# A macaron block on one core: operand and weight tiles 32 bytes further along from one tile to the next

## The chip, the cores and the metric

The kernel runs on one core of a Trainium2 chip. TensorE (PE) multiplies, VectorE (DVE) and ScalarE (ACT) do the element-wise work, GpSimd (POOL) does next to nothing here, and SyncE (SP) issues nearly all transfers. Data lies in SBUF, 128 partitions with one row of bytes each; a tile of 1,024 float32 takes 4,096 bytes of every partition's row. Matmul results go to PSUM, in banks of 512 float32 a partition. The metric is the device time in microseconds (us) of one execution; a lower one is better.

## What is computed

One layer of a streaming encoder, for 1,024 tokens of width 1,024, all in float32:

```python
h = x + 0.5 * swiglu_ffn(rmsnorm(x, norm_ffn1), ffn1_w_in, ffn1_w_out)     # D_FF = 2816
proj = rmsnorm(h, norm_mix) @ w_in                                         # q, k, v, g, p, two gates
ret = retention(rotary(q), rotary(k) * 256**-0.5, v)                       # 4 heads of 256, chunks of 64
ret = ret * rsqrt(mean(ret * ret) + eps) * silu(g)
pool_out = multiscale_pool(p, pool_w, pool_scale)                          # windows 2, 4, 8, 16
merged = sigmoid(gate0 + b0) * (ret @ w_ret_up) + sigmoid(gate1 + b1) * (pool_out @ w_pool_up)
h = h + merged @ w_out
h = h + 0.5 * swiglu_ffn(rmsnorm(h, norm_ffn2), ffn2_w_in, ffn2_w_out)
out = rmsnorm(h, norm_final)
```

## The kernel before

**Products in three parts.** [...] `split` writes the high part with ScalarE (L151) and the low part with VectorE (L152). A product of two operands is three matmuls that add up in one bank (`mm3`, L169 to L173): high weights by high data, high weights by low data, low weights by high data. In every one of them TensorE first loads a block of 128 x 128 of the stationary operand (the rows PEld LDWEIGHTS), while the matmul before it runs, and then streams the moving operand, 512 or 256 columns wide, past it. The trace names lines 171, 172 and 173 for the three.

**Where operands lie.** One pool, `sb`, holds everything that rotates; a tag is a row of equal buffers in it, and a new tile takes a buffer of its tag that has come free. The tags lie in SBUF one behind the other in the order in which they are first used. `mv` (L107, 28 buffers) holds moving operands: high part in the first half of the tile, low part in the second. `wt` (L110, 5 buffers) holds stationary ones, again both parts, each of four blocks of 128 columns. `raw` (4) holds weights as loaded, `t4` (9) and `tl` (4) results and spilled data, all of 4,096 bytes; `c2` (8) holds halves of 2,048 bytes. Some operands lie elsewhere: the blocks that `Next.blocks` (L337) makes for the lower level of the product scheme go to `tl` or `t4` as its callers say (L622), and `scores` (L1403) and the state of the retention put theirs into `t4`. In front of `sb` lies the pool `cp` with constants: among others the zeros and `ones_r`, a block of ones for sums over partitions.

**Fewer products.** A 2 x 2 scheme with seven products in place of eight (`strassen`) runs over all large products; pairs of neighbouring groups share a second level (`common`, L521). The groups read operands T and R of the normed input and weights L and S of sums of weight blocks, which VectorE and ScalarE prepare just ahead. In `prod` (L451, L543) the weights' tile stays over four (or two) steps and the moving tile changes with every step of three matmuls. In the second half of an FFN (`ffn_out`, `step`, L863) one weights' tile and one moving tile serve twelve matmuls.

**Order.** `Flow` runs a list of steps: each has a preparation and a body, and preparations run four steps (`LOOK`) ahead. Work that nobody waits for at once (scaling, gates, norms) stands in a second queue, of which one or two pieces are let in after each body. Each engine works through its instructions in the order that comes out of this; semaphores order the engines among each other.

**The zeros.** At the start VectorE fills `zero` (L187), and TensorE runs twelve matmuls on it (L193), which set the two banks that sums use and keep TensorE going while the first loads are on their way.

## Time and profile before

| | us |
|---|---|
| median of 3 runs | 2163.72 |
| lowest and highest | 2162.26, 2164.65 |
| span of the profiled execution (its time from the first to the last instruction) | 2160.9 |
| PE busy in it | 2148.0, 10,668 matmuls |
| DVE busy | 1870.0, 3,300 instructions |
| ACT busy | 1088.9, 2,047 instructions |

The profile is of one execution of its own. Its span leaves out what lies before the first and behind the last instruction, and is 2.8 us below the median. Busy time is the time in which an engine has an instruction; matmuls are pipelined, and each row gives a longer duration (0.39 us for 512 columns) than the distance to the next start. The distance between starts, from the view in order of time, tells how fast TensorE works. The first FFN fills the span to about 640 us, the projections go to about 1170, retention and pooling to about 1370, the branches' last products and the output product to about 1520, and the second FFN fills the rest.

### The profile page before, as it was taken

What the parts mean: (1) busy time and instruction counts of PE and PEld (TensorE: products, weight loads), DVE (VectorE), ACT (ScalarE), POOL (GpSimd) and SP (SyncE); (2) the same over time, 40 slices, a digit from 0 to 9 for tenths busy, and PEclk for the clock granted to TensorE, in tenths of its full rate; (3) what the DMA queues carried; (4) which work ended last, traced back from release to release, by engine and by line L of the source; (5) the groups of instructions that cost most, each with busy time, mean ns of one, the idle gap of its engine ahead of it and who ended that gap; (6) DMA issues with size and microseconds to landing.
All of it is one profiled execution on the core that took longest, in us unless ns stands there. A gap on an engine that the chain in (4) does not pass through costs nothing.

```text
span 2160.9 us, 29697 instructions
## 1 busy us (share of the span) xinstructions
PE 2148.0 (99%) x10668; PEld 1816.9 (84%) x10668; DVE 1870.0 (87%) x3300; ACT 1088.9 (50%) x2047; POOL 0.2 (0%) x4
## 2 busy tenths in 40 slices
PE   9999999999999999999999999999999999999998
PEld 7888888888888888888888898887888888888887
DVE  8799899998788798899767877899999989999784
ACT  8544444545656444444426754446644444455463
POOL 0000000000000000000000000000000000000000
PEclk9999999999999999999999999999999999999999
DMA  7232323596323333333485567624133232359532
GB/s 261 69 129 104 101 93 127 165 339 207 122 93 107 109 127 108 118 107 119 153 268 191 167 224 256 218 97 160 65 117 103 98 107 99 118 185 334 178 122 78
DMA packets 117828, 320.92 MB, mean 149 GB/s; under 512 B 12976, under 2 KB 17200, under 8 KB 117680
## 3 DMA queue, kind: packets, MB, share of 16 engines
q1 hardware_dynamic: 117104, 317.97, 43.4%
q8 instruction: 83, 1.36, 0.3%
q10 hardware_dynamic: 576, 1.05, 0.1%
q14 instruction: 65, 0.53, 0.1%
HBM read 228.27 MB, written 90.70 MB: 148 GB/s over the span
## 4 chain that ended last, share of the span: by engine, by line
PE 90%; DVE 7%; ACT 1%; issue 1%; DMA 1%; SPq 0%; ACTq 0%; DVEq 0%
PE c_b L171 2%; PE c_b L173 2%; PE c_b L172 2%; PE a_b L173 2%; PE a_b L171 2%; PE a_b L172 2%; PE c_e L173 2%; PE c_e L171 2%; PE c_e L172 2%; PE a_e L173 2%; PE a_e L171 1%; PE a_e L172 1%; PE bp6b L172 1%; PE bp6b L173 1%; PE bp6b L171 1%; PE c_a L172 1%
## 5 line engine op out<-in xcount | busy, mean ns | idle before, releaser
L172 PE MATMUL c_b<-n3T,c_wS 128*128 128x512 f32 x176 | 68.5, 389 | 0.0
L173 PE MATMUL c_b<-n3T,c_wS 128*128 128x512 f32 x176 | 68.5, 389 | 0.0
L171 PE MATMUL c_b<-n3T,c_wS 128*128 128x512 f32 x176 | 68.2, 390 | 0.0
L171 PE MATMUL a_b<-n1T,a_wS 128*128 128x512 f32 x168 | 65.5, 390 | 0.0
L172 PE MATMUL a_b<-n1T,a_wS 128*128 128x512 f32 x168 | 65.4, 389 | 0.0
L173 PE MATMUL a_b<-n1T,a_wS 128*128 128x512 f32 x168 | 65.4, 389 | 0.0
L173 PE MATMUL a_a<-n1R,a_wL 128*128 128x512 f32 x120 | 46.7, 390 | 0.8 <-DVE a_wL L152 0.8
L171 PE MATMUL a_a<-n1R,a_wL 128*128 128x512 f32 x120 | 46.8, 390 | 0.0
L172 PE MATMUL a_a<-n1R,a_wL 128*128 128x512 f32 x120 | 46.7, 389 | 0.0
L172 PE MATMUL c_a<-n3R,c_wL 128*128 128x512 f32 x112 | 43.7, 390 | 0.0
L171 PE MATMUL c_a<-n3R,c_wL 128*128 128x512 f32 x112 | 43.6, 389 | 0.0
L173 PE MATMUL c_a<-n3R,c_wL 128*128 128x512 f32 x112 | 43.6, 389 | 0.0
L173 PEld LDWEIGHTS c_b<-n3T,c_wS 128*128 128x128 f32 x176 | 33.0, 188 | 6.9
L171 PEld LDWEIGHTS c_b<-n3T,c_wS 128*128 128x128 f32 x176 | 33.0, 188 | 6.9
L172 PEld LDWEIGHTS c_b<-n3T,c_wS 128*128 128x128 f32 x176 | 33.0, 188 | 6.8
L171 PEld LDWEIGHTS a_b<-n1T,a_wS 128*128 128x128 f32 x168 | 31.5, 188 | 6.8 <-ACT a_v L471 0.3
L173 PEld LDWEIGHTS a_b<-n1T,a_wS 128*128 128x128 f32 x168 | 31.5, 188 | 6.6
L172 PEld LDWEIGHTS a_b<-n1T,a_wS 128*128 128x128 f32 x168 | 31.5, 188 | 6.5
L173 PE MATMUL c_e<-n3T,c_wS 128*128 128x512 f32 x88 | 35.1, 399 | 0.4 <-DVE c_wS L152 0.4
L171 PE MATMUL c_e<-n3T,c_wS 128*128 128x512 f32 x88 | 34.5, 393 | 0.0
L172 PE MATMUL c_e<-n3T,c_wS 128*128 128x512 f32 x88 | 34.4, 391 | 0.0
L173 PE MATMUL a_e<-n1T,a_wS 128*128 128x512 f32 x84 | 33.4, 398 | 0.9 <-DVE a_wS L152 0.9
(3058 smaller groups left out, 8076.2 us busy)
## 6 DMA issues: line engine op xcount, KB each, us to landing
c_ra<-in_f_in SPq DMA_DIRECT2D x22, 512.0 KB, 3.6
c_rb<-in_f_in SPq DMA_DIRECT2D x22, 512.0 KB, 4.1
a_ra<-in_f_in SPq DMA_DIRECT2D x21, 512.0 KB, 3.6
a_rb<-in_f_in SPq DMA_DIRECT2D x21, 512.0 KB, 4.4
t<-au SPq DMA_DIRECT2D x11, 512.0 KB, 2.6
b<-ag SPq DMA_DIRECT2D x11, 512.0 KB, 2.7
r<-au SPq DMA_DIRECT2D x11, 512.0 KB, 3.6
br<-r SPq DMA_DIRECT2D x11, 512.0 KB, 5.4
```

What stands on the lines that cost most here:

```text
L171: mm(dst, w[0], m[0], start=start, stop=False, skip_group_check=True)
L172: mm(dst, w[0], m[1], start=False, stop=False, skip_group_check=True)
L173: mm(dst, w[1], m[0], start=False, stop=stop, skip_group_check=True)
```

## The change

Tiles of `mv` and `wt` are allocated as rows of 1,032 float32 and used without the last eight, so that each buffer starts 4,128 bytes behind the one before it instead of 4,096: 32 bytes further along in a line, if the row of bytes is thought of as cut into lines of a power of two. The five places that take tiles of these tags go through one new function. The zeros move from a tile of their own in `cp` to a buffer of `c2`, which makes room for the extra bytes; as the first tile asked of `sb` they also put `c2` in front of the other tags. A tile of 32 bytes, `line`, is set aside in `cp` and never used. No other instruction is added, removed or moved in the program's text.

```diff
+    def staggered(tag, bufs, dtype, name):
+
+        return sb.tile([P, S + 8], dtype, tag=tag, bufs=bufs, name=name)[:, :S]
+
     def mv(name):
-        return sb.tile([P, 2, H], F32R, tag="mv", bufs=N_MV, name=name)
+        return staggered("mv", N_MV, F32R, name).rearrange("p (z c) -> p z c", z=2)
 
     def wt(name):
-        return sb.tile([P, 2, 4, P], F32R, tag="wt", bufs=N_WT, name=name)
+        return staggered("wt", N_WT, F32R, name).rearrange("p (z i c) -> p z i c", z=2, i=4)
...
-    zero = cp.tile([P, H], BF16, name="zero")
+    zero = sb.tile([P, 2 * H], BF16, tag="c2", bufs=N_C2, name="zero")[:, :H]
     nc.vector.memset(zero, 0.0)
...
     ones_r = cp.tile([P, P], F32R, name="ones_r")
+    cp.tile([P, 8], F32, name="line")
...
-                store[k // 2] = sb.tile([P, S], F32, tag="mv", bufs=N_MV, name=f"{name}{n}{k}")
+                store[k // 2] = staggered("mv", N_MV, F32, f"{name}{n}{k}")
...
-                self.row = sb.tile([P, S], F32, tag="mv", bufs=N_MV, name=f"{self.name}row")
+                self.row = staggered("mv", N_MV, F32, f"{self.name}row")
...
-                o = self.rows[n] = sb.tile([P, S], F32, tag="mv", bufs=N_MV, name=f"{self.name}o{n}")
+                o = self.rows[n] = staggered("mv", N_MV, F32, f"{self.name}o{n}")
```

## The prediction

> **What bounds the kernel now.** I read the page first (busy times, clock, chain), then the waits of TensorE, then the order of time of single matmuls, because the pitch from one matmul's start to the next is what this change can move.

> ```profile
> span 2160.9 us, 29697 instructions
> PE 2148.0 (99%) x10668; PEld 1816.9 (84%) x10668; DVE 1870.0 (87%) x3300; ACT 1088.9 (50%) x2047; POOL 0.2 (0%) x4
> PEclk9999999999999999999999999999999999999999
> PE 90%; DVE 7%; ACT 1%; issue 1%; DMA 1%; SPq 0%; ACTq 0%; DVEq 0%
> ```

> TensorE is busy 99% of the span, its clock is granted in full in all 40 slices, and it makes up 90% of the chain that ended last. The waits of TensorE are small; these are the longest:

> ```profile
> PE set L193 <- DVE zero L188: 1.2, 1, 1.2
> PE a_e L173 <- DVE a_wS L152: 0.9, 2, 0.5
> PE a_a L173 <- DVE a_wL L152: 0.8, 1, 0.8
> ```

> So the time is the number of matmuls times their pitch. A busy PE is not PE at its peak, so the pitch has to be read from starts. First 512 columns wide, in FFN 2 (time from the span's start, duration, instruction):

> ```profile
> 1604.89 0.39 PE L171 MATMUL c_a<-n3R,c_wL 128*128 128x512 f32 x1
> ...
> 1607.16 0.39 PE L172 MATMUL c_a<-n3R,c_wL 128*128 128x512 f32 x1
> ```

> Ten pitches in 2.27 us: 227 ns (226.7 over longer stretches). Now 256 columns wide; a row each at the start of a group and where it ends:

> ```profile
> 1592.50 0.28 PE L171 MATMUL c_b<-n3R,c_wx 128*128 128x256 f32 x1
> ...
> 1593.22 0.28 PE L171 MATMUL c_x<-n3R22y,c_ws 128*128 128x256 f32 x1
> ...
> 1593.94 0.28 PE L171 MATMUL c_b<-n3R,c_ws 128*128 128x256 f32 x1
> ...
> 1594.66 0.29 PE L171 MATMUL c_b<-n3R22y,c_wy 128*128 128x256 f32 x1
> 1594.78 0.28 PE L172 MATMUL c_b<-n3R22y,c_wy 128*128 128x256 f32 x1
> 1594.90 0.28 PE L173 MATMUL c_b<-n3R22y,c_wy 128*128 128x256 f32 x1
> 1595.02 0.28 PE L171 MATMUL c_b<-n3R22y,c_wy 128*128 128x256 f32 x1
> ...
> 1595.36 0.28 PE L171 MATMUL c_x<-n3R22y,c_ws 128*128 128x256 f32 x1
> ...
> 1596.04 0.39 PE L171 MATMUL c_e<-n3T,c_wL 128*128 128x512 f32 x1
> ```

> From 1592.50 to 1594.66 there are 18 pitches in 2.16 us: 120 ns. From 1595.36 to 1596.04 there are six in 0.68 us: 113 ns. The two groups named c_x<-n3R22y have the same line, shapes and engine, and differ in one thing: the moving operand. Line 622 puts the block y2, which the group at 1593.22 reads, into a buffer of the tag tl, and y3 and y4, read from 1594.66 on, into buffers of t4. In the program as built, counting bytes within a line of 128, every buffer of mv, wt, tl and c2 starts at 32, and every one of t4 and raw at 96. So where the moving operand and the weights that are loaded meanwhile lie at the same place of a line, a matmul of 256 columns takes 120 ns, and where they lie 64 bytes apart, 113.

> The difference of 512 and 256 columns at the same place is 226.7 - 120 = 106.7 ns for 256 columns, so both widths hold the same remainder that isn't columns: 120 - 106.7 = 13.3 ns a matmul, and half of it, 6.7, at 64 bytes apart. This remainder is what the change can reach.

> **The change part by part.**

> *The steps of 32 bytes.* Buffers of mv and wt become 4128 bytes instead of 4096. With five buffers of wt and 28 of mv, worked out in the order in which the tags are first used, wt starts at 64, 96, 0, 32, 64 and mv at 96, 0, 32, 64 and round again; t4, raw and c2 start at 0, tl at 96. Offsets inside a tile are multiples of 512 bytes and change nothing. Put on the trace's order of matmuls, buffers as they are now, the moving operand and the next weights are then 0, 32, 64 and 96 bytes apart in about a quarter of the cases each; today 8,041 matmuls of 512 columns are practically all at 0, and of 2,334 of 256 columns four fifths. (The count by width is mine from the trace; it agrees with the page: if all 10,668 were one or the other, 2148.0 us would need 8,136 wide ones.)

> What 32 and 96 bytes cost is not in the trace, nor is a settled 512 at 64. Bounds of the remainder: 0 and 13.3 ns. I take 6.7, the only row that isn't at the same place, for all three. Then the mean remainder is (13.3 + 3 x 6.7) / 4 = 8.3. The wide ones gain 5.0 ns: 8,041 x 5.0 = 40.2 us. The narrow ones go from a mean of 118.6 to 115.0: 8.4 us. Sum: 48.6 us faster if every matmul runs at its settled pitch.

> *Settling.* It won't: the trace shows what a change of place costs. In the rows below two matmuls read ones_r (at 96) between operands at 32.

> ```profile
> 1557.00 0.39 PE L172 MATMUL c_e<-n3T,c_wL 128*128 128x512 f32 x1
> 1557.23 0.39 PE L173 MATMUL c_e<-n3T,c_wL 128*128 128x512 f32 x1
> 1557.45 0.62 PE L238 MATMUL n30b<-n30dg,ones_r 128*128 128x512 f32 x2
> 1557.91 0.40 PE L171 MATMUL c_b<-n3R,c_wS 128*128 128x512 f32 x1
> 1558.15 0.39 PE L172 MATMUL c_b<-n3R,c_wS 128*128 128x512 f32 x1
> 1558.38 0.40 PE L173 MATMUL c_b<-n3R,c_wS 128*128 128x512 f32 x1
> 1558.61 0.39 PE L171 MATMUL c_b<-n3R,c_wS 128*128 128x512 f32 x1
> 1558.84 0.39 PE L172 MATMUL c_b<-n3R,c_wS 128*128 128x512 f32 x1
> ```

> From 1557.23 to 1558.84 seven pitches take 1.61 us, where seven settled ones take 1.587: 23 ns for two changes, 12 each. After the change the distance alters some 3,450 times, about every third matmul (the moving tile changes with i in prod, L451): at most 3,450 x 12 = 41 us. At least nothing: at 1594.66 the move to 64 bytes apart costs no more than 120 ns for three matmuls and gains from the fourth. I take 15 us, a good third: most of the excess lies behind a return to the same place, which is one change in four, and the steps of FFN out, with one pair of tiles for twelve matmuls (step, L863), settle. Left: 33.6 us.

> *VectorE.* When TensorE gets faster, VectorE is late next. It is nearly full in two stretches:

> ```profile
> 1400.00:1650.00 250.00, 248.93 (x1141) 206.27 (x1140) 244.27 (x432) 138.52 (x253) 0.00 (x0) 1.00 0.30 104
> 1900.00:2000.00 100.00, 100.00 (x481) 84.28 (x481) 97.05 (x167) 51.16 (x93) 0.00 (x0) 1.00 0.79 274
> ```

> (Columns: stretch, length, busy PE, PEld, DVE, ACT.) In the first, VectorE has 5.7 us free of 250, and a gain of 1.6% would ask for 3.9 of them; queues rarely use all, so I take off 2 us there and 1 in the second. Nothing is lost if it keeps pace, at most the 6 us that both stretches would gain. VectorE's and ScalarE's own instructions don't get slower by place: the same shape takes

> ```profile
> L152 DVE TENSOR_TENSOR c_wS<-c_S,c_wS 128x512 fp32r<-128x512 f32 x46 | 31.4, 685 | 1.2 <-ACT c_wS L151 1.2
> L716 DVE TENSOR_TENSOR cu<-cu,n3rb 128x512 f32<-128x512 f32 x44 | 30.1, 685 | 0.0
> L151 ACT CAST a_wS<-a_S 128x512 fp32r<-128x512 f32 x45 | 27.1, 620 | 13.3 <-PE a_a L173 5.0 <-DVE a_S L429 3.7 <-PE a_e L173 2.5
> L151 ACT CAST a_wL<-a_ra 128x512 fp32r<-128x512 f32 x30 | 18.4, 621 | 17.6 <-PE a_e L173 5.6 <-DVE ag L710 4.8 <-DMA a_ra<-in_f_in 2.6
> ```

> with all operands at 32, all at 96, or a mix: 685 and 620 ns either way.

> *The zeros and the empty line.* The same memset and twelve warm-up matmuls write and read another address. Cost 0: the twelve end near 6.5 us under the first loads, and c2 is first wanted again later. Without that cover a wait for the buffer would cost at most the 1.2 us of the first wait above. The tile called line takes no instruction. Order and number of all other instructions stay, so queues and transfers move only with TensorE; no transfer is among TensorE's waits.

> Sum, against the span: -48.6 + 15 + 3 = -31 us, to 2130; the median of the runs lies 2.8 us above the span, so 2133.

> [...]

> **The rivals.**

> *The beat is lost (slower).* Today all operands lie alike, and TensorE falls into a steady 226.7 ns. If distances that change every third matmul keep it unsettled, the pitch is that of the rows from 1557.23 on, 1.61 / 7 = 230 ns: 8,041 x 3.3 = 27 us more, the narrow ones staying at 120: 2190. For it: the seven rows; against it: 113 ns once settled. It decides as soon as the mean pitch of the wide ones, unsettled, is above 226.7.

> *Only the narrow ones respond.* No settled 512 at another place is in the trace. Then 8.4 us: 2155.

> *VectorE becomes the bound.* If TensorE gains but waits for weights through FFN 1 and FFN 2, half of 31 us is left: 2148. Against it: three waits of under 1 us with VectorE at 98%.

> *The change does nothing.* The 7 ns come from something else than place, such as the traffic on the tag's buffers: 2163.7. Against it: same line, same shape, 2 us apart.

> **How the numbers follow.** Forecast 0.55, narrow alone 0.14, VectorE 0.06, nothing 0.05, beat lost 0.20. Below and above 0.2% (4.3 us, about what a measurement of this kernel can tell from no change): faster 0.75, same 0.05, slower 0.20. The forecast's own range is 2100 to 2158. With a remainder of 0 at the three other places and no settling cost the time is near 2065 (10 ns on each wide one, 8.6 on each narrow one), with 12 ns for every change and no gain 2205; from 2098 to 2176 about 2 in 10 is left out.

> **What would show it.** In the changed kernel's order of time, 512-wide starts less than 226.7 ns apart, mixed values inside a group of twelve, settled ones in the steps named bp and dp; 256-wide ones near 115; busy VectorE above 98% from 1400 on and TensorE's waits on L152 longer. Wrong: starts 230 ns apart and wandering (beat lost), or 226.7 throughout (place without effect).

## The result and the profile after

The changed kernel takes 2201.4 us (median of 4 runs, 2200.26 to 2201.88) against 2162.99 for the kernel before on the same chip (2161.79 to 2164.65): a ratio of 1.0173, interval 1.0159 to 1.0188. It is 38 us slower; the forecast was 2133, 31 us faster.

From the page of the changed kernel: span, busy times, the granted clock in 40 slices, and the chain's shares by engine.

```profile
span 2199.7 us, 29697 instructions
PE 2186.0 (99%) x10668; PEld 1816.3 (83%) x10668; DVE 1876.4 (85%) x3300; ACT 1089.9 (50%) x2047; POOL 0.2 (0%) x4
PEclk9999999999999999999999999999999999999999
PE 95%; DVE 3%; DMA 1%; ACT 1%; issue 0%; SPq 0%; DVEq 0%; ACTq 0%
```

The counts of instructions are those of before and the granted clock is 0.999, as before; PE's busy time went from 2148.0 to 2186.0 us, nearly as much as the span (2160.9 to 2199.7). The waits of TensorE are as small as they were (engine, tile and line | what it waited for | us in total, times, longest):

```profile
PE set L197 <- DVE zero L192: 1.2, 1, 1.2
PE a L175 <- ACT n1R L159: 0.8, 1, 0.8
PE a_a L177 <- DVE a_wL L156: 0.8, 1, 0.8
```

So the matmuls themselves follow one another more slowly. In the order of time (start, duration, instruction) the group c_a<-n3R,c_wL in the second FFN has 48 matmuls of 512 columns; first the kernel before, its first start and the first start of the group that follows, then the changed kernel:

```profile
1601.49 0.39 PE L171 MATMUL c_a<-n3R,c_wL 128*128 128x512 f32 x1
...
1612.38 0.39 PE L171 MATMUL c_e<-n3T,c_wS 128*128 128x512 f32 x1
```

```profile
1591.88 0.39 PE L175 MATMUL c_a<-n3R,c_wL 128*128 128x512 f32 x1
...
1603.00 0.40 PE L175 MATMUL c_e<-n3T,c_wS 128*128 128x512 f32 x1
```

10.89 us and 11.12 us: 226.9 and 231.7 ns a matmul. The narrow groups that the prediction read, in the changed kernel:

```profile
1621.84 0.28 PE L175 MATMUL c_x<-n3R22y,c_ws 128*128 128x256 f32 x1
...
1622.56 0.28 PE L175 MATMUL c_b<-n3R,c_ws 128*128 128x256 f32 x1
...
1623.95 0.28 PE L175 MATMUL c_x<-n3R22y,c_ws 128*128 128x256 f32 x1
...
1624.65 0.40 PE L175 MATMUL c_e<-n3T,c_wL 128*128 128x512 f32 x1
```

Six of 256 columns take 0.72 and 0.70 us, 120 and 117 ns; before it was 120 and 113.

Over the whole span I took the distance from each matmul's start to the next in the order of time (distances above 260 and 150 ns, which are pauses, left out) and set beside it the addresses of the program as built. "Distance" below is the start of the moving operand less the start of the weights that are loaded meanwhile, those of the next matmul, counted within 256 bytes.

```
mean pitch, ns         before     after
512 columns            227.04     232.34
256 columns            118.69     117.97
pauses, us beyond the pitch      15.8   13.5

after, 512 columns, by distance in bytes
0      32     64     96     128    160    192    224
231.2  232.3  230.8  233.5  232.0  233.3  232.3  233.3
```

8,041 matmuls x 5.3 ns = 42.6 us more, 2,334 x 0.72 = 1.7 us less, 2.3 us less of pauses: 38.6 us, where the spans differ by 38.8. No distance is as fast as the old mean (227.04), and the matmuls at distance 0 are slower too (231.2) while the distance keeps changing. Where it stays, in the groups of twelve of the first FFN's second half, they nearly come back: from the seventh matmul of a pair of tiles on, distance 0 has 227.5 ns, and the others 228.8 (64 bytes) to 234.4 (160).

VectorE, which the prediction thought late next, has more room, not less. The stretch of the changed kernel that holds the work of the old 1400 to 1650 (stretch, length, busy PE, PEld, DVE, ACT):

```profile
1425.00:1680.00 255.00, 253.93 (x1140) 206.29 (x1139) 245.83 (x431) 139.05 (x253) 0.00 (x0) 1.00 0.29 102
```

96.4% instead of 97.7%, with nearly the same instructions (431 of VectorE, 432 before) in 255 us that took 250.

### The profile page after: what moved, and what is told of

It reads as the page before. It is cut to its first block, busy times and chain, and to the rows that moved or that the text cites. A ratio compares the mean times of both kernels' runs of the same rounds, so it can differ in the third digit from the quotient of the medians.

```text
span 2199.7 us, 29697 instructions
## 1 busy us (share of the span) xinstructions
PE 2186.0 (99%) x10668; PEld 1816.3 (83%) x10668; DVE 1876.4 (85%) x3300; ACT 1089.9 (50%) x2047; POOL 0.2 (0%) x4
## 4 chain that ended last, share of the span: by engine, by line
PE 95%; DVE 3%; DMA 1%; ACT 1%; issue 0%; SPq 0%; DVEq 0%; ACTq 0%
PE a_b L177 2%; PE a_b L175 2%; PE a_b L176 2%; PE c_b L175 2%; PE c_b L177 2%; PE c_b L176 2%; PE c_e L177 2%; PE c_e L175 2%; PE c_e L176 2%; PE a_e L177 2%; PE a_e L176 2%; PE a_e L175 2%; PE a_a L177 1%; PE c_a L177 1%; PE c_a L176 1%; PE a_a L176 1%
## 5 line engine op out<-in xcount | busy, mean ns | idle before, releaser
L177 PE MATMUL c_e<-n3T,c_wS 128*128 128x512 f32 x88 | 35.0, 398 | 0.3 <-DVE c_wS L156 0.3
L177 PE MATMUL c_e<-n3T,c_wL 128*128 128x512 f32 x88 | 34.7, 395 | 0.0
L175 PE MATMUL c_e<-n3T,c_wL 128*128 128x512 f32 x88 | 34.7, 395 | 0.0
L175 PE MATMUL c_e<-n3T,c_wS 128*128 128x512 f32 x88 | 34.7, 395 | 0.0
```

The costliest lines, as they stand in the source:

```text
L175: mm(dst, w[0], m[0], start=start, stop=False, skip_group_check=True)
L177: mm(dst, w[1], m[0], start=False, stop=stop, skip_group_check=True)
```

## The experiments

Two theories stood at the start. *Place*: the pitch depends on where the moving operand lies against the weights that are loaded meanwhile, and other places than the same one are slower for 512 columns. *Change*: a constant distance would do no harm or good, and what costs is that the distance alters every third matmul (the rival "The beat is lost").

### The step taken out, the rest left

```diff
-        return sb.tile([P, S + 8], dtype, tag=tag, bufs=bufs, name=name)[:, :S]
+        return sb.tile([P, S], dtype, tag=tag, bufs=bufs, name=name)[:, :S]
```

> The changed kernel with tiles of 4096 bytes again; the zeros stay in c2, c2 stays first, and the empty line stays. If the step of 32 bytes is the whole cause (all theories of place or change of place): 2163 us, as before, give or take 2, wide matmuls 226.7 ns apart. If the zeros, the order of the tags or the empty line cost something: up to 2201.

2163.4 us, ratio 0.9999 (0.999 to 1.0009); 512 columns 227.04 ns. The zeros in c2, the tags' order and the empty line cost nothing, and that mv, wt and tl now all start at 64 instead of 32, counted within 256 bytes, doesn't matter: it isn't the place as such.

### One constant distance: 32, 64 and 128 bytes

The kernel before, with an unused tile ahead of mv and one ahead of tl that brings tl and c2 back (behind the # stand the sizes of the other two runs):

```diff
+    def place(tag, size):
+        if tag not in gap:
+            gap[tag] = sb.tile([P, size // 4], F32, tag="gap" + tag, bufs=1, name="gap" + tag)
+
     def mv(name):
+        place("mv", 32)      # 64, 128
...
     def tl(name):
+        place("tl", 224)     # 192, 128
```

> The kernel before with mv alone moved by 32 bytes, one and the same distance for all its tiles. Place theory (only operands at the same place of a line fall into the short beat; settled or not, 32 bytes apart means the 233.4 ns that the changed kernel's trace shows behind the sixth matmul of one pair of tiles): 7,500 wide matmuls x 6.7 ns = 50 us more, about 2213. Change theory (the loss comes from distances that change every third matmul): a constant distance settles, so 2163 or less, down to 2123 with the 6.7 ns saved that the prediction took.

> The same with 64 bytes. Place theory: 228.8 ns as in the changed kernel's trace for 64 apart, 7,500 x 2.1 = 16 us more, and 970 narrow ones 6.7 ns faster: 2163 + 16 - 6 = 2173. Change theory: it settles, 2163 down to 2115 (226.7 - 6.7 = 220 ns for the wide ones).

> The same with 128 bytes, which tells how long a line is. If it is 128 bytes, as the prediction had it, nothing changes: 2163. If it is 256 bytes: the changed kernel's trace has 232.8 ns for 128 apart, so 7,870 x 6.1 = 48 us more, 2211. Change theory: 2163 or less whatever the line.

| constant distance | us (median) | ratio | 512 columns, ns | 256 columns, ns |
|---|---|---|---|---|
| 0 (before) | 2163.95 | | 227.04 | 118.69 |
| 32 | 2207.94 | 1.0206 (1.0191 to 1.0222) | 233.22 | 118.18 |
| 64 | 2185.74 | 1.01 (1.0083 to 1.0117) | 230.26 | 118.67 |
| 128 | 2204.75 | 1.0189 (1.0174 to 1.0204) | 232.67 | 118.10 |

The same group of 48, at 32, 64 and 128 bytes, in the order of time of these three kernels:

```profile
1598.39 0.39 PE L179 MATMUL c_a<-n3R,c_wL 128*128 128x512 f32 x1
...
1609.60 0.39 PE L179 MATMUL c_e<-n3T,c_wS 128*128 128x512 f32 x1
```

```profile
1621.80 0.39 PE L179 MATMUL c_a<-n3R,c_wL 128*128 128x512 f32 x1
...
1632.79 0.39 PE L179 MATMUL c_e<-n3T,c_wS 128*128 128x512 f32 x1
```

```profile
1594.54 0.40 PE L179 MATMUL c_a<-n3R,c_wL 128*128 128x512 f32 x1
...
1605.70 0.39 PE L179 MATMUL c_e<-n3T,c_wS 128*128 128x512 f32 x1
```

11.21, 10.99 and 11.16 us: 233.5, 229.0 and 232.5 ns where before has 226.9. Nothing changes from matmul to matmul here. At 32 and 128 bytes the kernel is still as slow as after the change, or slower, and at 64 bytes it loses more than half as much. *Change*, by which a constant distance does no harm, falls. That 128 bytes cost nearly as much as 32 shows in addition that the pitch of 512 columns doesn't come back after 128 bytes: 232.67 ns there, 227.04 at 0. *Place* was off at 64 bytes, 2186 for 2173: 512 columns have 230.3 ns where I took 228.8, and 256 columns gave nothing back, though the same distance had given 113 ns in one group of the kernel before (v by sm, in the retention).

### Every distance, with nothing beside it

A stretch ahead of the work: rows of 36 matmuls on zeros at a constant distance, in two widths, after the loop that sets the sums' banks. `px` are two tiles of mv and `pw` one of wt, filled with zeros; `at` gives the columns by which the moving operand and the weights are moved, 4 bytes each.

```diff
...
+    def probe(name, n, at, count=36):
+        b = bank(name)
+        for k in range(count):
+            m, w = at(k)
+            mm(b[:, :n], pw[:, k % 4 * P + w : k % 4 * P + w + P], px[k % 2][:, m : m + n], start=True, stop=True)
+
+    for n in (H, HD):
+        for m, w in ([(d, 0) for d in range(0, 64, 4)] + [(64, 0), (2, 0), (0, 0), (1, 0)] + [(8, 8), (0, 8), (32, 32), (0, 32)]
+                     + [(d, 0) for d in (32, 0, 16, 48, 8, 0)]):
+            probe(f"p{n}_{m}_{w}", n, lambda k: (m, w))
+        for s in (8, 16, 32, 64):
+            probe(f"p{n}s{s}", n, lambda k: (k // 3 * s % 256, 0), 72)
```

> The kernel before with a stretch of its own ahead of the work: rows of 36 matmuls on zeros (adding to the time, leaving nothing out), the moving operand and the weights a constant number of bytes apart in each, VectorE and ScalarE idle; then four rows of 72 in which the distance steps by 32, 64, 128 or 256 bytes every third matmul. If the place alone sets the pitch: 512 columns 226.7 ns at 0, 233.3 at 32, 230 at 64, 232.7 at 128, at 256 columns 120 at 0 and 118 elsewhere; the same with both moved by 32 bytes as at 0 with neither moved; the row whose distance steps by 256 bytes like 0. If the other engines' writes into the displaced buffers are what costs, every row has one pitch, 226.7 and 120, since nothing else runs here.

The kernel ran once, in 2641.4 us. In the view by stretches (stretch, length, busy PE, PEld, DVE, ACT), each stretch below runs from the first start of a row to the first start of the next row, as the trace has them: its length over 36 is the row's pitch (the number in brackets counts neighbours that reach into the stretch). In order: 512 columns at distances 32, 64, 224, 240, 0; weights moved by 32 bytes and the moving operand not; both moved by 128; then 64 and 32 once more; then 256 columns at 112, 192, 192 again, 0.

```profile
22.41:30.82 8.41, 8.41 (x38) 6.75 (x36) 8.41 (x15) 1.27 (x3) 0.00 (x0) 1.00 0.47 185
39.21:47.47 8.26, 8.26 (x38) 6.76 (x37) 1.48 (x3) 0.00 (x0) 0.00 (x0) 1.00 0.00 0
122.92:131.32 8.40, 8.40 (x38) 6.76 (x36) 0.00 (x0) 0.00 (x0) 0.00 (x0) 1.00 0.00 0
131.32:139.49 8.17, 8.17 (x38) 6.76 (x37) 0.00 (x0) 0.00 (x0) 0.00 (x0) 1.00 0.01 2
156.09:164.28 8.19, 8.19 (x38) 6.76 (x36) 0.00 (x0) 0.00 (x0) 0.00 (x0) 1.00 0.00 0
180.96:189.36 8.40, 8.40 (x37) 6.76 (x36) 0.00 (x0) 0.00 (x0) 0.00 (x0) 1.00 0.00 0
189.36:197.56 8.20, 8.20 (x37) 6.76 (x36) 0.00 (x0) 0.00 (x0) 0.00 (x0) 1.00 0.00 0
222.52:230.78 8.26, 8.26 (x37) 6.76 (x36) 0.00 (x0) 0.00 (x0) 0.00 (x0) 1.00 0.01 2
239.17:247.56 8.39, 8.39 (x38) 6.75 (x36) 0.00 (x0) 0.00 (x0) 0.00 (x0) 1.00 0.00 0
352.13:356.21 4.08, 4.08 (x38) 4.08 (x37) 0.00 (x0) 0.00 (x0) 0.00 (x0) 1.00 0.00 0
373.27:377.36 4.09, 4.09 (x38) 4.09 (x37) 0.00 (x0) 0.00 (x0) 0.00 (x0) 1.00 0.00 0
437.58:441.82 4.24, 4.24 (x39) 4.24 (x38) 0.00 (x0) 0.00 (x0) 0.00 (x0) 1.00 0.01 4
398.75:403.07 4.32, 4.32 (x39) 4.32 (x37) 0.00 (x0) 0.00 (x0) 0.00 (x0) 1.00 0.00 0
```

233.6, 229.4, 233.3, 226.9, 227.5, then 233.3 and 227.8, then 229.4 and 233.1; narrow 113.3, 113.6, 117.8, 120.0. Moving the weights alone by 32 bytes costs (233.3 ns for 227.5), moving both by 128 doesn't (227.8): in these rows the pitch follows the distance. VectorE and ScalarE are idle from the sixth row on; under the first five they still prepare the first steps of the work. The pitch from the 13th matmul of each row on (where a distance stands in two rows with different results, both):

```
distance, bytes  0      16     32     48     64     80     96     112
512 columns      226.7  231.6  233.3  233.4  228.8  231.1  233.1  231.4
256 columns      120.0  118.7  116.7  118.3  117.8  119.8  120.0  113.4

distance, bytes  128          144    160    176    192          208    224    240
512 columns      232.1/233.5  233.3  234.3  233.3  233.4        234.8  233.4  226.7
256 columns      118.9/120.0  118.6  117.3  119.4  113.4/117.8  119.3  118.1  117.1
```

The values are close to those of the whole kernels (233.2 at 32, 230.3 at 64, 232.7 at 128), though nearly all rows ran with VectorE and ScalarE idle, and the row at 32 has 233.3 ns with VectorE busy all the time as well as with it idle: in these rows the other engines' writes aren't the cause. Distances of 8 and 4 bytes are no better (233.3 and 236.6 ns; 120.0 and 123.4 for 256 columns). The row whose distance steps by 256 bytes every third matmul has 226.7 ns, those with steps of 32, 64 and 128 have 232.6, 231.6 and 232.3, near the 232.3 of the changed kernel. Weighted with the changed kernel's counts, the row's values give 232.0 of its 232.3 ns: the places are nearly all of the loss, and 0.3 ns, 2.5 us, is left for the changes of distance. That is a net figure: beside the row at the same distance, 0 and 64 lose by the changes (231.2 for 226.7 ns, 230.8 for 228.8), and 160 and 192 gain (233.3 for 234.3, 232.3 for 233.4).

### Each part alone, and a step of 256 bytes

In `staggered` the step becomes a matter of the tag: none for mv and 256 bytes for wt; none and 32; 32 and none.

```diff
-        return sb.tile([P, S + 8], dtype, tag=tag, bufs=bufs, name=name)[:, :S]
+        return sb.tile([P, {"mv": S, "wt": S + 64}[tag]], dtype, tag=tag, bufs=bufs, name=name)[:, :S]
...
+        return sb.tile([P, {"mv": S, "wt": S + 8}[tag]], dtype, tag=tag, bufs=bufs, name=name)[:, :S]
...
+        return sb.tile([P, {"mv": S + 8, "wt": S}[tag]], dtype, tag=tag, bufs=bufs, name=name)[:, :S]
```

> The change with the step of wt at 256 bytes and that of mv at none, so that buffers are as unequally spaced as after the change, but all operands at the same place of a line of 256 bytes. Place (line of 256 bytes): 512 columns stay at 227.0 ns and the time at 2164. If uneven spacing itself, or a line longer than 256 bytes, is what costs: 512 columns at 231 to 233, 2195 to 2207.

> The change's step for wt alone: the distance stays for a whole tile of weights, twelve matmuls or so, and is 32, 64, 96, 128 or 160 bytes in a fifth of the cases each. Place: a mean of 232.6 ns by the pitches of the runs with constant distances, 8,041 x 5.6 = 45 us more, 1 to 2 us back from 256 columns: 2207. If the changes of distance are what costs, they are four times rarer than after the change, and a quarter of its 38 us is left: 2173.

> The change's step for mv alone: the distance changes with every third matmul and takes all eight multiples of 32 about equally. Place: as after the change, a mean of 232 ns, 2200. If each part costs by itself and they add up to the 38 us of both: this and the run with wt alone share it, 2183 on average.

A step of 256 bytes: 2163.93 us, ratio 1.0001 (0.9991 to 1.001), 512 columns 227.07 ns; the group of 48:

```profile
1603.36 0.39 PE L175 MATMUL c_a<-n3R,c_wL 128*128 128x512 f32 x1
...
1614.24 0.39 PE L175 MATMUL c_e<-n3T,c_wS 128*128 128x512 f32 x1
```

226.7 ns a matmul. Uneven spacing costs nothing here (227.07 ns, before 227.04), and as steps of 256 bytes cost nothing and a distance of 128 does, it is the distance counted within 256 bytes that the pitch follows in these kernels. wt alone by 32: 2203.25, ratio 1.0184 (1.0167 to 1.0201), 232.53 ns. mv alone by 32: 2200.92, ratio 1.017 (1.0155 to 1.0186), 232.36 ns. Either part costs what both together cost, as *place* says, and the rarer changes of distance with wt alone save nothing. The parts don't add up.

### Looking for a faster place

The kernel before with an unused tile of 192 bytes ahead of tl; the step of 256 bytes again, with wt's tiles used from byte 16 on; and this with an unused tile of 128 bytes ahead of tl.

```diff
+    gap = []
+
     def tl(name):
+        if not gap:
+            gap.append(sb.tile([P, 48], F32, tag="gap", bufs=1, name="gap"))
         return sb.tile([P, S], F32, tag="tl", bufs=N_TL, name=name)
...
-        return sb.tile([P, S + 8], dtype, tag=tag, bufs=bufs, name=name)[:, :S]
+        if tag == "wt":
+            return sb.tile([P, S + 64], dtype, tag=tag, bufs=bufs, name=name)[:, 4 : S + 4]
+        return sb.tile([P, S], dtype, tag=tag, bufs=bufs, name=name)
```

> The kernel before with the buffers of tl, moving operands of 256 columns alone, put 192 bytes further on by an unused tile, which is where t4 lies already. Place: some 600 matmuls of 256 columns go from 120.0 ns to 113.3 if they settle at once, 115.2 as those from t4 do; 512 columns stay. 2.9 us less (0 to 4.0): 2161. No effect of place on narrow ones: 2163.8.

> All buffers at the same place of a line of 256 bytes but wt, which lies 16 bytes further on, so that nearly all moving operands are 240 bytes ahead of the weights. By the pitches of the run with a stretch of its own: 512 columns 226.65 ns at 240 as at 0, 335 of them at 16 with 231.6 (1.6 us more); about 1,580 of 256 columns at 117.1 in place of 119.8 (4.3 us less), 234 from t4 at 176 with 119.3 in place of 115.2 (1 us more). Sum: 1.7 us less, 2162. If any distance but 0 costs in the whole kernel: 2200.

> As the run with wt 16 bytes further on, and tl so that its moving operands are 112 bytes ahead of the weights, where the row of 256 columns had 113.3 ns from the start: 605 matmuls by another 3.8 us. Sum: 4 us less than before (up to 5.5), 2160. If the narrow ones don't settle between other work, 2162.

tl at 192: 2161.69 against 2163.70 us, ratio 0.9991 (0.9982 to 0.9999): 2.0 us less, where 2.9 (0 to 4.0) was expected. The mean of 256 columns went from 118.69 to 117.22 ns, 512 columns stayed (226.99). This is the one version below the kernel before, by less than the 0.2% that a measurement can tell for certain.

wt at 16: 2198.3, ratio 1.0158 (1.0145 to 1.0172), not 2162. With tl at 112 too: 2196.47, ratio 1.0155 (1.0141 to 1.0169), not 2160; the narrow ones at 112 had 119.3 ns, not 113.3. The reason shows in the same group of 48, in two places of the kernel with wt at 16, both at distance 240 throughout:

```profile
1590.83 0.39 PE L177 MATMUL c_a<-n3R,c_wL 128*128 128x512 f32 x1
...
1601.71 0.39 PE L177 MATMUL c_e<-n3T,c_wS 128*128 128x512 f32 x1
```

```profile
1628.61 0.40 PE L177 MATMUL c_a<-n3R,c_wL 128*128 128x512 f32 x1
...
1639.81 0.40 PE L177 MATMUL c_e<-n3T,c_wS 128*128 128x512 f32 x1
```

10.88 and 11.20 us: 226.7 and 233.3 ns. At this one distance the trace has two pitches, and a stretch mostly holds one of them: of 589 pieces of twelve matmuls at a constant distance of 240, 119 had a mean of 227 or 228 ns (rounded) and 470 one of 233 or 234. Of the 62 stretches in which 24 or more such matmuls follow one another without a pause, 47 are slow throughout (the longest 1,055 matmuls), 14 fast throughout (the longest 514), and one changes its pitch on the way. The row of 36 in the stretch of its own had the fast one, 226.7. In the stretch of its own every row of 512 columns at distance 0 came to 226.7; of the other distances 240 alone did, and the whole kernel shows that it need not.

## Why the prediction was wrong

*What bounds the kernel* was right: TensorE's pitch. The span followed it to within 1 us (38.6 worked out, 38.8 measured), and no wait took its place.

*The step that failed* is "I take 6.7, the only row that isn't at the same place, for all three". The row is of 256 columns and comes from groups in which 113 ns held for six matmuls. It was carried over to 512 columns, where the prediction had said itself that no settled row existed. Measured at that group's distance (192 bytes, counted within 256) in the row of zeros: 512 columns 233.4 ns, a remainder of 20 by the prediction's own way of counting (233.4 less 2 x 106.7) instead of 6.7. The assumption behind it, that both widths hold the same remainder and places shrink it for both, is wrong: away from 0 the narrow ones gain 0 to 3 ns in most rows and the wide ones lose 2 to 8 (240 aside). The term "-40.2 us" was +42.6.

*The bounds* failed with it. "0 and 13.3 ns" made the value of the same place the upper end, so that a loss by place was shut out without a row that excluded it; the range ended at 2176. The rows gave no reason for that: 13.3 was worked out at one place, and no row showed what 512 columns cost at another. The prediction did give a slower kernel 0.20, but through the changes of distance, and its 2190 lay outside the range.

*The line.* I counted places in lines of 128 bytes. A distance of 128 took 2204.75 us and steps of 256 took 2163.93, against some 2164 before: what counts as the same place here comes round every 256 bytes. So only an eighth of the cases, not a quarter, stayed at the same place.

*The narrow ones.* Forecast 115.0 ns on average and 8.4 us less; measured 117.97 and 1.7 us less. 113 ns is not the only pitch at its distance: at 192 bytes two rows with the same place had 113.4 and 117.8, and the kernel with tl at 192 had 115.5 there.

*Settling* (+15 us) was mis-sized: by the rows' values the changes of distance cost some 2.5 us net. *VectorE* (+3 us), an estimate of mine that VectorE wouldn't use all the time it has free, which no run shows: not reached, as TensorE got slower. *The zeros and the line*, cost 0: right (0.9999).

*The rival that came nearest*, the lost beat (2190), had the right sign and nearly the right pitch, 230 for 232.3, and the wrong cause: it put the loss on the changes of distance, and constant distances of 32 and 128 bytes cost as much as the change itself, or more. That it came near was luck. The other rivals, at 2164 or below, fall with the 2201.4 measured.

## What to carry to other kernels

In this kernel, where TensorE's pitch at 512 columns sets the time and weights are loaded for every matmul, the versions whose 512-wide moving operands nearly all lie at the same offset as the weights modulo 256 bytes took 2161.69 to 2163.95 us, and 32 bytes of an unused tile cost 2% (2207.94). In a kernel like it, look at these offsets after any change of tile sizes, tags or constants, and time both. A pitch read from a short run at one width was no pitch for the other width here, and no bound either (113 ns at 256 columns, 233.4 at 512, at the same distance): measure the whole set of places with a stretch of its own, from more than one starting point, before a sum is built on one row. Where an effect has been seen at one value only, the range has to reach to its other side.

## What was unexpected of the hardware

The pitch of 226.7 ns is the exception. Of the sixteen multiples of 16 bytes in the rows of zeros, two gave it, 0 and 240, and 240 in the whole kernel only at times. In the changed kernel's groups of twelve the pitch at other distances wanders in short cycles that repeat to within 1 ns or so, such as 226, 229, 232 ns at 64 bytes and 235, 232, 235, 231 at 224; the rows of zeros have 228.8 and 233.4 ns at these distances. The widths disagree about good places: of these sixteen, distance 0 is the best for 512 columns (226.7 ns) and, with 96 bytes and 128 in one of its rows, the worst for 256 (120.0 ns, down to 113.4 elsewhere). And one constant distance, 240, showed two pitches, 226.7 and 233.3 ns, in stretches of up to 514 and 1,055 matmuls with no pause between them.
